# A first stage with its loads in another order, x turned by VectorE, five raw weight buffers and weights split ahead of scalings

## The chip, the cores and the metric

The kernel runs on one core of a Trainium2 chip. The metric is the time of one execution in microseconds on the device; the time of before is the median of three runs. A core has a matrix engine (TensorE, PE in the profile; its weight loads are PEld), three engines for other arithmetic (VectorE = DVE, ScalarE = ACT, GpSimd = POOL), a SyncE (SP) whose queue issues the DMAs, and DMA engines. Each engine works off its own queue of instructions; semaphores make them wait for each other. SBUF is the on-chip memory, PSUM the small memory that matmuls write to.

## The reference

One layer of a streaming encoder, for a prompt of 512 frames and a sample of 64 frames, width 2048, all in float32. Cut to what matters here:

```python
mod = jax.nn.silu(c) @ w_ada + b_ada                     # (2048) @ (2048, 6*2048), for two c
sh1, sc1, g1, sh2, sc2, g2 = split(mod, 6)
h = rmsnorm(x, norm1) * (1 + sc1) + sh1
proj = h @ w_in                                          # then gated linear attention, gated DeltaNet
x = x + g1 * (concat(o_a, o_b) @ w_out)
h = rmsnorm(x, norm2) * (1 + sc2) + sh2
x = x + g2 * conv_ffn(h)                                 # w_up, causal depthwise conv, w_down
y = rmsnorm(x, final_norm)
```

The first stage of the kernel, which the change touches, computes x transposed and its row norms, the first two of the six modulation parts (sh1 and sc1), h, and the first six column blocks of `h @ w_in` together with 32 narrow columns of it.

## The kernel before

Float32 products are made of two parts each: a weight tile w is split into wh (w rounded to the matmul's short form, by ACT) and wl = w - wh (by DVE), h likewise into hh and hl, and one product is wh hh + wh hl + wl hh, that is six matmuls of 288 columns (`mm6`, L744 and L746) for a tile of 128 rows by 128 columns. The 576 frames stand as two halves of 288 (256 of the prompt and 32 of the sample).

The stage is the method `head`. It works in this order.

- **x.** `x_load` brings x in five blocks of 128 rows (the fifth, the sample, has 64), each as four loads of 512 columns. `x_square` sums squares on ACT, `x_norm` makes 1/rms (DVE and POOL), `x_turn` transposes by PE in groups of four 128x128 tiles into a PSUM tile (tag g, two buffers), which is copied out to `xT` by ACT for even groups and by DVE for odd ones. `x_diag` puts the norms on a diagonal, and `x_lengths` multiplies by ones so that rb holds each frame's 1/rms in all partitions.
- **Modulation.** The 16 tiles of the width are taken in six groups of 2, 2, 3, 4, 3 and 2 tiles (`GROUPS`). `modulation(g)` multiplies silu(c) with the columns of `w_ada` of group g, eight steps (for part 1 and then part 0 of the modulation, four k-steps each); group 0 goes one step at a time, the others two. Its tiles come in buffers `hraw` (nine of 512 KB); `ada_fill` issues the next loads as soon as steps free buffers. After four steps the row is copied out by DVE (rw), transposed by PE (L2410), summed and joined with the bias (L991, L1167) and, for the scale part, with norm1 (L1173).
- **h.** `scale(k)` makes tmp = xT * s1 * rb on DVE (L765); `make(k)` adds the shift and rounds to hh on ACT (L772) and makes hl on DVE (L775).
- **Products.** The six column blocks (`EARLY`) are taken in three pairs for each group; pair j = 3 g + e/2 is pair e/2 of group g. `pair_load` brings a pair's raw weights into a buffer of tag raw (three of them; 256, 384 or 512 KB for groups of 2, 3 and 4 tiles), `w_ahead(n)` issues the loads of all pairs below n, and `pair_split` makes wh (ACT, L1139) and wl (DVE, L1141) in three buffers each. For each group the loop runs the first pair (e = 0) tile by tile together with the narrow product (L1262), then the pairs e = 2 and e = 4; `product` advances the next group's modulation step by step, and at its fourth step issues two scalings of the next group. The sums over groups are kept in SBUF (`sum_early`, L1150 and L1164).

What sets the order: all loads of this stage are issued by SP in the order in which the program traces them, and an issue whose buffer isn't free holds up those behind it. ACT and DVE run their queues in an order that follows the trace too, except that `high_priority(offset=80)` moves instructions ahead and `issue_after(ins)` (`after`) holds them behind `ins` on its engine. In `x_turn` the transposes are held behind the last modulation step (`summed`) and the copies behind a given square (`squared`). For groups from 1 on, the next group's narrow split and first pair's split are traced at the start of e = 4, and scalings are held behind them (`split_of`).

The buffers of tag xr (two of 512 KB in the same pool as raw) aren't used in this stage before its last group.

Of the kernel before, what the change touches and what calls it, by code (L numbers as in the profile page):

```python
# [16 lines left out]
P = 128  # L17
# [97 lines left out]
class Kern:  # L115
# [714 lines left out]

    def raw_late(self):

        pool, tag = self.raws.pop(0)
        self.raws.append((pool, tag))
        return pool.tile([P, 1024 if pool is not self.xp else NJ * P], F32, tag=tag, name=self.name("raw"))
# [21 lines left out]
    def head(self, pool):  # L857
# [5 lines left out]
        xt, ms, squared = {}, {}, []  # L863
# [9 lines left out]
        def x_square(b):  # L873
            n = P if b < 4 else TS
            ms[b] = pool.tile([P, 8], F32, tag="ms4", bufs=5, name=self.name("ms4"))
            for q in range(4):
                A.activation(junk[:n], xt[b][q][:n], AF.Square, scale=float(D) ** -0.5, accum_out=ms[b][:n, q:q + 1])
                squared.append(last())
# [18 lines left out]
        def x_turn(b):  # L897
            n = P if b < 4 else TS
            per = 4 if b < 4 else 8
            for k0 in range(0, KD, per):  # L900
                ps = self.pgt()[:, 0]
                for k in range(k0, k0 + per):
                    with self.tc.issue_after(summed[0]) if summed else nullcontext():
                        T.transpose(ps[:, (k - k0) * n:(k - k0 + 1) * n], xt[b][k // 4][:n, k % 4 * P:(k % 4 + 1) * P],
                                    self.c["ident"][:n, :n])
                even = k0 // per % 2 == 0
                put = (lambda o, x: A.activation(o, x, AF.Copy)) if even else V.tensor_copy
                ahead = 4 * b + (8 if k0 // per < 2 else 10)
                with self.tc.issue_after(squared[min(len(squared), ahead) - 1]):
                    if b < 4:  # L910
                        put(xT[:, k0:k0 + per, b // 2, (b % 2) * P:(b % 2 + 1) * P], ps.rearrange("p (k t) -> p k t", k=per))
                    else:
                        for h in range(2):
                            put(xT[:, k0:k0 + per, h, HP:HT], ps.rearrange("p (k h t) -> p k h t", k=per, h=2)[:, :, h])
# [9 lines left out]
        x_load(2)  # L924
# [35 lines left out]
        def modulation(g):  # L960
# [3 lines left out]
            for n0 in range(8 * g, 8 * g + 8, together):  # L964
# [13 lines left out]
                summed[:] = [last]  # L978
# [51 lines left out]
        for b in range(5):  # L1030
            if b < 4:
                x_norm(b + 1)
# [3 lines left out]
            x_diag(b)  # L1036
# [1473 lines left out]
```

## Time and profile before

| | |
|---|---|
| time, median of three runs (lowest, highest) | 2729.54 us (2727.57, 2734.78) |
| the profiled execution's own time | 2729.87 us |
| its span, first to last instruction | 2728.2 us |
| mean granted clock of PE | 0.997 |
| HBM read and written | 400.38 MB and 84.04 MB |
| DMA, mean over the span | 179 GB/s |

The span is what the profiler saw between the first and the last instruction; the execution's own time has 1.7 us more around it. "Granted clock" is the share of full speed that the throttle gave PE. In a table of stretches, each row gives the stretch, its length, then for each engine the busy time and the number of instructions, PE's granted clock, the mean busy share of the DMA engines (it can be over 1, since packets overlap) and what they moved in GB/s. In the timeline a row has the start, the time until the last of the merged instructions ended, engine, line, operation, out<-in, the number of instructions, and in brackets the engine's idle time before it and what ended it.

The chain of work that ended last, over the whole span, by engine:

```profile
PE 82%; DVE 8%; DMA 4%; issue 3%; ACT 2%; SPq 0%; POOL 0%; ACTq 0%; DVEq 0%; POOLq 0%
```

The first stage's loads, from the DMA issues up to 200 us: 40 loads of w_ada of 512 KB and 32 of 384 KB, x in 16 loads of 256 KB and four of 128 KB, and the weight pairs in loads of 128 to 256 KB, two for each pair.

### The profile page before, as it was taken

How to read it: one execution, taken by the hardware profiler on the slowest of the kernel's cores; microseconds unless marked ns; L12 is line 12 of the kernel's file. 1: busy time of each engine (PE TensorE's matmuls, PEld its weight loads, DVE VectorE, ACT ScalarE, POOL GpSimd, SP SyncE). 2: the span in 40 equal slices, each digit the busy share in tenths (PEclk: the TensorE clock that was granted, in tenths of full speed). 3: DMA queues.
4: the chain of work that ended last, by engine and by line, in shares of the span. 5: the costliest groups of instructions: out<-in, count | busy, mean ns of one | idle time of the engine just before them, and what ended most of it. 6: DMA issues, size and time to landing. Idle time of an engine off the chain costs nothing.

```text
span 2728.2 us, 52233 instructions
## 1 busy us (share of the span) xinstructions
PE 2682.6 (98%) x20208; PEld 2620.1 (96%) x20208; DVE 2292.2 (84%) x3747; ACT 1295.6 (47%) x2317; POOL 477.8 (18%) x461
## 2 busy tenths in 40 slices
PE   7999999999999999999999999999999999999998
PEld 5799999999999999999999999999999999999998
DVE  4579899988989895688999999999999976888996
ACT  4246454555554442554545454545454544333453
POOL 0001010110001000001333333333333300000241
PEclk9999999999999999999999999999999999999999
DMA  9986565555565583634555555555555595674762
GB/s 303 347 256 186 151 171 161 168 171 147 154 180 164 159 270 90 179 98 120 162 168 163 167 163 167 165 165 167 163 168 162 165 312 184 197 223 121 237 181 82
DMA packets 646203, 487.84 MB, mean 179 GB/s; under 512 B 66601, under 2 KB 568356, under 8 KB 645956
## 3 DMA queue, kind: packets, MB, share of 16 engines
q1 hardware_dynamic: 632852, 471.04, 57.5%
q10 hardware_dynamic: 13104, 13.47, 1.7%
q8 instruction: 159, 2.61, 0.4%
q14 instruction: 88, 0.72, 0.1%
HBM read 400.38 MB, written 84.04 MB: 178 GB/s over the span
## 4 chain that ended last, share of the span: by engine, by line
PE 82%; DVE 8%; DMA 4%; issue 3%; ACT 2%; SPq 0%; POOL 0%; ACTq 0%; DVEq 0%; POOLq 0%
PE g L744 17%; PE bank L1881 16%; PE bank L1880 16%; PE bank L1882 16%; PE g L746 8%; PE bank L2414 4%; DVE wl L1790 2%; PE bank L744 1%; PE bank L2410 1%; DVE m L2368 1%; DVE wl L2395 1%; DMA raw<-in_w_out_dram 1%; PE bank L973 1%; DMA raw<-in_w_in_dram 1%; DVE slot L2076 1%
## 5 line engine op out<-in xcount | busy, mean ns | idle before, releaser
L1881 PE MATMUL bank<-slot,wh 128*128 128x290 f32 (+1 forms) x3584 | 1067.3, 298 | 0.0
L1880 PE MATMUL bank<-slot,wh 128*128 128x290 f32 (+1 forms) x3584 | 1063.1, 297 | 1.0 <-DVE v L1903 0.6
L1882 PE MATMUL bank<-slot,wl 128*128 128x290 f32 (+1 forms) x3584 | 1060.3, 296 | 1.3 <-DVE wl L1790 1.2
L1882 PEld LDWEIGHTS bank<-slot,wl 128*128 128x128 f32 x3584 | 680.0, 190 | 2.9 <-DVE wl L1790 2.5
L1880 PEld LDWEIGHTS bank<-slot,wh 128*128 128x128 f32 x3584 | 675.4, 188 | 5.2 <-issue 4.4
L1881 PEld LDWEIGHTS bank<-slot,wh 128*128 128x128 f32 x3584 | 677.0, 189 | 0.1
L744 PE MATMUL g<-hh,wh 128*128 128x288 f32 x2048 | 470.1, 310 | 1.6 <-DVE kt L2395 0.7
L1788 ACT ACTIVATE wh<-raw 128x1024 fp32r<-128x1024 f32 (+1 forms) x304 | 280.7, 924 | 348.5 <-PE bank L1881 325.2
L746 PE MATMUL g<-hh,wl 128*128 128x288 f32 x2048 | 442.7, 297 | 2.3 <-DVE wl L1141 2.3
L744 PE MATMUL g<-hl,wh 128*128 128x288 f32 x2048 | 442.8, 297 | 0.3 <-DVE hl L775 0.2
L1790 DVE TENSOR_TENSOR wl<-raw,wh 128x1024 fp32r<-128x1024 f32 (+1 forms) x304 | 374.2, 1231 | 69.0 <-ACT wh L1788 66.0
L1788 ACT ACTIVATE wh<-s 128x1024 fp32r<-128x1024 f32 (+1 forms) x228 | 211.0, 927 | 296.5 <-PE bank L1881 136.6
L744 PEld LDWEIGHTS g<-hh,wh 128*128 128x128 f32 x2048 | 325.5, 189 | 15.9 <-issue 10.4
L746 PEld LDWEIGHTS g<-hh,wl 128*128 128x128 f32 x2048 | 330.8, 189 | 4.2 <-DVE wl L1141 2.7
L744 PEld LDWEIGHTS g<-hl,wh 128*128 128x128 f32 x2048 | 330.6, 189 | 2.7 <-issue 1.9
L1790 DVE TENSOR_TENSOR wl<-s,wh 128x1024 fp32r<-128x1024 f32 (+1 forms) x228 | 251.0, 1102 | 13.7 <-ACT wh L1788 12.5
L2395 ACT ACTIVATE wh<-raw 128x1024 fp32r<-128x1024 f32 x135 | 143.1, 1062 | 185.6 <-PE g L744 145.1
L2004 POOL TENSOR_TENSOR j<-j,j 128x288 f32<-128x288 f32 (+1 forms) x120 | 186.0, 1557 | 84.0 <-ACT j L2008 82.1
L2395 DVE TENSOR_TENSOR wl<-raw,wh 128x1024 fp32r<-128x1024 f32 x135 | 165.9, 1229 | 35.5 <-ACT wh L2395 35.2
L2395 DVE SCALAR_TENSOR_TENSOR acc<-aw,ct,acc 128x512 f32<-128x512 f32 x264 | 187.7, 743 | 0.0
L2395 DVE SCALAR_TENSOR_TENSOR acc<-xr,ct,acc 128x512 f32<-128x512 f32 x216 | 154.2, 748 | 0.0
L2076 DVE TENSOR_TENSOR slot<-bank,slot 128x288 f32<-128x288 f32 x184 | 83.0, 451 | 33.7 <-PE bank L1882 32.6
(317 smaller groups left out, 3269.4 us busy)
## 6 DMA issues: line engine op xcount, KB each, us to landing
raw<-in_w_up_dram SPq DMA_DIRECT2D x176, 512.0 KB
raw<-in_w_in_dram SPq DMA_DIRECT2D x100, 512.0 KB
raw<-in_w_down_dram SPq DMA_DIRECT2D x128, 320.0 KB
slot<-cd SPq DMA_DIRECT2D x140, 288.0 KB
aw<-in_w_ada_dram SPq DMA_DIRECT2D x74, 512.0 KB
cd<-j SPq DMA_DIRECT2D x120, 288.0 KB
xr<-in_w_ada_dram SPq DMA_DIRECT2D x54, 512.0 KB
hraw<-in_w_ada_dram SPq DMA_DIRECT2D x40, 512.0 KB
```

Source lines behind the costliest of these rows:

```text
L744: T.matmul(ps[:, h if bank is None else bank, :n], wh, x[:, h, :n], start=f, stop=False)
L746: T.matmul(ps[:, h if bank is None else bank, :n], wl, ah[:, h, :n], start=False, stop=stop)
L973: T.matmul(ps[32 * k:32 * k + 32, :w], cs[:, k0 + k], got[n][k // per][:, k % per], start=(n == together - 1 + 8 * g + 4 * (1 - mi)), stop ...
L1788: self.nc.scalar.activation(hi, src, AF.Copy)
L1790: self.nc.vector.tensor_tensor(lo, src, hi.bitcast(F32), op=ALU.subtract)
L1880: T.matmul(ps, wh[:, j], hi, start=(c < 3 and j == 0), stop=False, skip_group_check=True)
L1881: T.matmul(ps, wh[:, j], lo, start=False, stop=False, skip_group_check=True)
L1882: T.matmul(ps, wl[:, j], hi, start=False, stop=(j == n - 1), skip_group_check=True)
L2004: minus = lambda out, a, b: G.tensor_tensor(out, a, b, op=ALU.subtract)
L2076: V.tensor_tensor(dst, ps, dst, op=ALU.add)
L2395: r = f(*a, **kw)
L2414: return self.engine.matmul(out, *a, **kw)
```

## The change

- The constants are loaded first, then all five blocks of x (with the two c vectors behind the second), and only then `b_ada`, the norms, `w_ada` and weights. Of group 0, six `w_ada` tiles are issued, then weight pair 0 and the narrow weights, then the other two tiles, then pairs 1 and 2.
- A Silu of a small constant runs on ACT before the squares.
- `x_turn` copies the groups of the four prompt blocks by DVE alone, those of the sample block by ACT alone, and the holding behind `summed` and `squared` is gone. The modulation steps of group 0 come later in the trace: the first after block 3 is turned, the second before the lengths, three after them, the last three after the first two scalings.
- Weight pairs take five buffers: of each five, three of tag raw and two of tag xr. `w_ahead` runs two pairs further ahead throughout.
- In each group, the next group's narrow weights are loaded at the start; their split and the split of the next group's first pair are traced at the fourth modulation step, ahead of the two scalings, and the scalings are held behind them. Before, both splits stood at the start of e = 4.

```diff
+    def raw_early(self):
+        self.n_early = getattr(self, "n_early", -1) + 1
+        return self.xr() if self.n_early % 5 in (3, 4) else self.raw()
...
                 for k in range(k0, k0 + per):
-                    with self.tc.issue_after(summed[0]) if summed else nullcontext():
-                        T.transpose(ps[:, (k - k0) * n:(k - k0 + 1) * n], xt[b][k // 4][:n, k % 4 * P:(k % 4 + 1) * P],
-                                    self.c["ident"][:n, :n])
-                even = k0 // per % 2 == 0
-                put = (lambda o, x: A.activation(o, x, AF.Copy)) if even else V.tensor_copy
-                ahead = 4 * b + (8 if k0 // per < 2 else 10)
-                with self.tc.issue_after(squared[min(len(squared), ahead) - 1]):
...
+                    T.transpose(ps[:, (k - k0) * n:(k - k0 + 1) * n], xt[b][k // 4][:n, k % 4 * P:(k % 4 + 1) * P],
+                                self.c["ident"][:n, :n])
+                if b < 4:
+                    V.tensor_copy(xT[:, k0:k0 + per, b // 2, (b % 2) * P:(b % 2 + 1) * P], ps.rearrange("p (k t) -> p k t", k=per))
+                else:
+                    for h in range(2):
+                        A.activation(xT[:, k0:k0 + per, h, HP:HT], ps.rearrange("p (k h t) -> p k h t", k=per, h=2)[:, :, h], AF.Copy)
...
+        self.load_consts(self.cp, LONG)
         x_load(0)
-        self.load_consts(self.cp, LONG)
         x_load(1)
         v_load, v_turn = self.load_vectors()
         v_load(0)
-        x_load(2)
+        for b in range(2, 5):
+            x_load(b)
+        warm = pool.tile([P, 8], F32, tag="ms4", bufs=6, name=self.name("ms4"))
+        A.activation(warm, self.mhalf, AF.Silu)
+        for b in range(2):
+            x_square(b)
         v_turn(0)
...
-                    w_ahead(3 if g == 1 else 3 * g - 2)
+                    w_ahead(3 * g)
...
-        first, summed, self.split_of = modulation(0), [], None
-        ada_ahead(2)
-        x_load(3)
-        x_load(4)
-        ada_ahead(4)
+        first, self.split_of = modulation(0), None
         v_load(1)
-        ada_ahead(7)
+        ada_ahead(6)
         w_ahead(1)
         nar = self.narrow_load(*GROUPS[0])
-        x_square(0)
-        x_norm(0)
-        x_square(1)
+        ada_ahead(8)
+        w_ahead(3)
         for b in range(5):
-            if b < 4:
-                x_norm(b + 1)
             if b < 3:
                 x_square(b + 2)
             x_turn(b)
-            x_diag(b)
+            x_norm(b)
             if b > 0:
+                x_diag(b - 1)
+            if b == 3:
                 next(first)
-            if b == 3:
-                v_turn(1)
+        x_diag(4)
+        next(first)
         x_lengths()
+        v_turn(1)
+        for _ in range(3):
+            next(first)
         for k in range(2):
             scale(k)
...
-        w_ahead(2)
+        w_ahead(5)
...
+            nar_raw = None if end else self.narrow_load(*GROUPS[g + 1])
+
+            def split_next():
+                nonlocal nar
+                nar = self.narrow_split(pool, nar_raw)
+                begun.append(self.pair_split(*raws[3 * g + 3]))
+                self.split_of = last()
...
                     if stepped == 4 and not end:
+                        split_next()
                         for i in range(2):
                             scale(m0 + nm + i)
...
-                w = begun.pop(0) if begun else self.pair_split(*raws[3 * g + e // 2])
+                w = begun.pop(0) if e == 0 or g == 0 else self.pair_split(*raws[3 * g + e // 2])
...
-                            w_ahead(3 * g + 3)
+                            w_ahead(3 * g + 5)
...
-                    if e == 4 and not end and j == 0:
-                        nar = self.narrow_split(pool, self.narrow_load(*GROUPS[g + 1]))
-                        begun.append(self.pair_split(*raws[3 * g + 3]))
-                        self.split_of = last()
...
-                            w_ahead(3 * g + e // 2 + 3)
+                            w_ahead(3 * g + e // 2 + 5)
...
     def pair_load(self, offs, k0, n):
-        raw, w = self.raw(), n * P
+        raw, w = self.raw_early(), n * P
```

More of the change, by code (lines that the diff above doesn't have):

```diff
@@ L862, in head @@
         slot = lambda: self.hslot(places.pop(0), [P, 512])
-        xt, ms, squared = {}, {}, []
+        xt, ms = {}, {}
         last = lambda: nc.cur_bb.bb.instructions[-1]
@@ L874, in x_square @@
             n = P if b < 4 else TS
-            ms[b] = pool.tile([P, 8], F32, tag="ms4", bufs=5, name=self.name("ms4"))
+            ms[b] = pool.tile([P, 8], F32, tag="ms4", bufs=6, name=self.name("ms4"))
             for q in range(4):
                 A.activation(junk[:n], xt[b][q][:n], AF.Square, scale=float(D) ** -0.5, accum_out=ms[b][:n, q:q + 1])
-                squared.append(last())
         def x_norm(b):
@@ L977, in modulation @@
                     got[n] = None
-                summed[:] = [last]
                 ada_fill()
@@ L1016, in make @@
             self.h.append((hh, hl))
-        first, summed, self.split_of = modulation(0), [], None
-        ada_ahead(2)
-        x_load(3)
-        x_load(4)
-        ada_ahead(4)
+        first, self.split_of = modulation(0), None
         v_load(1)
-        ada_ahead(7)
+        ada_ahead(6)
         w_ahead(1)
         nar = self.narrow_load(*GROUPS[0])
-        x_square(0)
-        x_norm(0)
-        x_square(1)
+        ada_ahead(8)
+        w_ahead(3)
         for b in range(5):
-            if b < 4:
-                x_norm(b + 1)
             if b < 3:
```

4 lines of the change are left out of this document (removed).

## The prediction

> **What bounds the kernel now.** I read the page first (busy shares), then the table of stretches, then the PE waits of the first stage.
>
> ```profile
> PE 2682.6 (98%) x20208; PEld 2620.1 (96%) x20208; DVE 2292.2 (84%) x3747; ACT 1295.6 (47%) x2317; POOL 477.8 (18%) x461
> ```
>
> ```profile
> core 0: us, PE busy (x) PEld busy (x) DVE busy (x) ACT busy (x) POOL busy (x), PEclk, DMA share, GB/s
> 0.00:37.00 37.00, 21.17 (x162) 14.26 (x162) 13.78 (x45) 23.75 (x60) 3.78 (x12) 1.00 0.97 305
> 37.00:60.00 23.00, 22.34 (x185) 17.31 (x186) 8.87 (x23) 8.26 (x17) 0.26 (x1) 0.93 0.89 297
> 60.00:98.00 38.00, 35.20 (x273) 23.75 (x271) 21.79 (x48) 6.04 (x12) 0.59 (x2) 1.00 1.04 363
> 98.00:107.00 9.00, 6.95 (x41) 5.95 (x34) 4.79 (x9) 3.68 (x6) 0.00 (x0) 0.81 1.07 361
> 107.00:160.00 53.00, 53.00 (x449) 45.72 (x448) 33.04 (x69) 13.59 (x25) 0.21 (x1) 1.00 0.92 304
> 160.00:2728.20 2568.20, 2543.90 (x19113) 2513.11 (x19111) 2209.89 (x3557) 1240.26 (x2200) 472.94 (x445) 1.00 0.57 170
> ```
>
> TensorE (PE) is busy 98% of the span. The first stage (head) fills about 0 to 160 us; behind it PE is busy 2543.9 of 2568.2 us, and the change edits nothing there. So I take whatever the head gains or loses as passing to the end one for one. In the head there are three kinds of time to win. Before the first product (37 us) PE is idle 37.00 - 21.17 = 15.8 us. From 37 to 107 it is idle 0.66 + 2.80 + 2.05 = 5.5 us. From 107 to 160 it never rests: nothing can be won there. The third kind is half clock:
>
> ```profile
> 34.00:37.00 3.00, 0.63 (x6) 0.20 (x2) 2.42 (x8) 0.88 (x3) 0.00 (x0) 1.00 1.00 331
> 37.80:41.20 3.40, 3.40 (x19) 2.99 (x21) 2.09 (x5) 1.18 (x3) 0.00 (x0) 0.50 1.09 382
> 99.20:102.60 3.40, 1.67 (x12) 1.21 (x10) 2.42 (x3) 1.06 (x1) 0.00 (x0) 1.00 1.02 360
> 102.70:106.10 3.40, 3.40 (x16) 3.40 (x17) 1.10 (x4) 1.81 (x4) 0.00 (x0) 0.50 1.09 379
> ```
>
> Twice the granted clock is 0.50 for 3.4 us, each time right behind a stretch in which PE was busy half the time or less. Each costs half of 3.4 us, 1.7 us. So the most that can be won from 37 us on is 5.5 + 2 x 1.7 = 8.9 us, and the DMA column warns that not all of it is PE's own: from 60 to 107 us the DMA engines are full (share 1.04 and 1.07).
>
> ```profile
> PE g L746 <- DVE wl L1141: 2.3, 2, 2.1
> PE bank L2410 <- DVE rw L984: 1.5, 1, 1.5
> PE ps_nar L1262 <- ACT hh L772: 1.5, 1, 1.5
> PE g L744 <- ACT wh L1139: 0.5, 2, 0.3
> ```
>
> These are PE's longest waits from 37 to 162 us (total, times, longest): the split weights (wh, wl), the modulation row (rw), and hh, which is the start itself.
>
> **The start (0 to 37 us).**
>
> ```profile
> 12.27 1.28 ACT L931 ACT_TABLE_LOAD   x1
> 27.55 0.47 SPq L948 DMA_DIRECT2D hraw<-in_w_ada_dram  x1
> 28.01 0.64 PE L973 MATMUL bank<-hraw,cs 128*32 128x256 f32 x8
> 32.26 1.93 PE L973 MATMUL bank<-hraw,cs 128*32 128x256 f32 x32
> 33.05 1.81 DVE L765 SCALAR_TENSOR_TENSOR tmp<-xT,s,rb 128x512 f32<-128x512 f32 x4 [0.67 <-ACT rb L895]
> 34.78 0.41 DVE L984 COPY rw<-bank 128x256 f32<-128x256 f32 x1
> 36.12 1.81 ACT L772 ACTIVATE hh<-tmp,mod 128x512 fp32r<-128x512 f32 x4 [2.44 <-DVE mod L1167]
> ```
>
> ```profile
> L911 DVE COPY xT<-g 128x512 f32<-128x512 f32 x8 | 5.5, 690 | 7.8 <-PE g L904 7.8
> L907 ACT ACTIVATE xT<-g 128x512 f32<-128x512 f32 x8 | 4.7, 585 | 1.5 <-PE g L904 1.5
> ```
>
> The first product needs the eight modulation steps of group 0, hence their last load, issued at 27.55. Ahead of it stand all of x, the constants, c, b_ada, the norms, seven w_ada tiles, one weight pair and the narrow weights. Behind the change the same set stands ahead of it, only x earlier and w_ada later; the DMA share is already 0.97 up to 37 us. So that load lands when it landed, about 31 us by issue order and bytes, and the step that uses it still comes at about 32.3. Hence these edits cost or gain nothing:
> - The eight ACT copies become DVE copies: 8 x 0.69 = 5.5 us more on DVE, 4.7 us off ACT. DVE then has 13.78 + 5.5 = 19.3 us in 37, hidden under the loads. With that cover gone it would be up to 5.5 us.
> - The early Silu removes the 1.28 us table load in mid-stage; ACT isn't what ends last here. At most 1.28 us.
> - x and constants first: the two w_ada tiles that stood ahead of x's last blocks come behind, so the x chain (squares, lengths, rb) ends sooner, but it has to wait for the modulation.
>
> What does change is the tail. Now four steps run at 32.26 in 1.93 us, and rw waits until tmp ends at 34.86 although PE was done at 34.19. With the lengths done before, the steps follow their loads, and behind the last load stands one step of 0.64 us: 1.3 us less, and 0.5 us less for rw. Against it: PE now does little between the transposes and the last step, and both rows above show such a stretch being paid with half clock. I put 1.3 us for that (three quarters of one 1.7 us window). **Term 1: -1.8 + 1.3 = -0.5 us**, bounds -3.5 (x's earlier end also pulls the loads forward) and +2 (two half-clock windows, or DVE behind with x).
>
> The rule that speaks against the change here: the Trainium skill, TensorE: Matmul & The Clock Gate, Part 1, says that PE's clock falls to half after an idle window of about 3.4 us and recovers only after one busy window. This trace agrees with the length and the factor (3.40 us at 0.50). By the rule a sparser PE before the start gives one more such window, and the sum would be 0.4 us worse than with my three quarters.
>
> **Deeper weight loads and the middle (60 to 98 us).**
>
> ```profile
> 57.65 1.50 PE L973 MATMUL bank<-hraw,cs 128*32 128x384 f32 x16
> 59.97 3.98 SPq L948 DMA_DIRECT2D hraw<-in_w_ada_dram  x8
> 64.00 3.86 SPq L1126 DMA_DIRECT2D raw<-in_w_in_dram  x4
> 66.47 0.53 PE L746 MATMUL g<-hh,wl 128*128 128x288 f32 x2 [2.06 <-DVE wl L1141]
> 68.47 5.89 SPq L948 DMA_DIRECT2D hraw<-in_w_ada_dram  x8
> 77.50 3.62 SPq L1126 DMA_DIRECT2D raw<-in_w_in_dram  x2
> 81.37 6.25 SPq L948 DMA_DIRECT2D hraw<-in_w_ada_dram  x8
> 96.61 1.92 PE L973 MATMUL bank<-hraw,cs 128*32 128x512 f32 x16
> ```
>
> At 64.00 DVE scales the next x tiles (1.8 us) while wl waits behind it, and PE loses 2.06 us at 66.47. Splitting first removes that wait, and pairs loaded two ahead remove the waits on wh. But what is late next? PE frees the w_ada buffers at 57.65, the second half of group 2's tiles goes out at 59.97, then weights and group 3's tiles without a pause, the last batch by 87.6. In issue order these are 8 x 384 + 16 x 512 KB of w_ada and 1 MB of pairs, 12.6 MB; at 363 GB/s they take 34.7 us, so the last lands at about 95, and PE uses it at 96.61. This chain of full DMAs fixes the use at 96.61, whatever PE saves in between: PE would wait there instead. So the 2.80 us of this stretch count as nothing. The deeper loads even add to it: between 59.97 and the last batch now go weight pairs 5, 6 and 7 (256 + 384 + 384 KB), then pairs 7, 8 and 9 (384 + 384 + 512 KB), 256 KB more, 0.26 MB / 363 GB/s = 0.7 us. **Term 2: +0.7 us**; bounds -2.8 (the DMAs have slack after all) and +2.
>
> SP's queue: the narrow load moves from late in a group to its start, ahead of 16 w_ada issues; two issues of under 0.5 us each, with a DMA queue in backlog. Nothing. Were the queue empty they would cost 1 us a group.
>
> **The end of the full-DMA stretch (98 to 107 us).**
>
> ```profile
> 87.66 5.91 SPq L1126 DMA_DIRECT2D raw<-in_w_in_dram  x4
> 97.97 0.84 ACT L1139 ACTIVATE wh<-raw 128x768 fp32r<-128x768 f32 x1 [11.19 <-DMA raw<-in_w_in_dram]
> 99.60 1.06 ACT L1139 ACTIVATE wh<-raw 128x1024 fp32r<-128x1024 f32 x1 [0.79 <-DMA raw<-in_w_in_dram]
> 100.69 1.23 DVE L1141 TENSOR_TENSOR wl<-raw,wh 128x1024 fp32r<-128x1024 f32 x1 [0.89 <-ACT wh L1139]
> 101.83 0.68 DVE L984 COPY rw<-bank 128x512 f32<-128x512 f32 x1
> 102.57 1.07 PE L2410 MATMUL bank<-consts,rw 128*128 128x128 f32 x4 [1.53 <-DVE rw L984]
> ```
>
> Pairs 8 and 9 were issued at 87.66 behind the full queue, so wh, wl and then rw came late: 2.05 us of idle PE, and it brought the second half-clock window, 1.7 us. With the change pairs 8 and 9 are issued a group earlier, and the split of pair 9 comes early in its group: I count all 3.7 us, less 0.5 us, since the next w_ada tiles (group 4) still come through a queue that holds 0.7 us more. **Term 3: -3.2 us**; bounds -3.7 and 0.
>
> **Sum:** -0.5 + 0.7 - 3.2 = -3.0 us. The profiled execution took 2729.87 us (span 2728.2 and 1.7 around it); the median of the three runs, 2729.54, is 0.3 lower. Forecast from the median: **2726.5 us**, by -0.11%. 0.3% (8.2 us) is about what a measurement of this kernel tells from no change.
>
> **The rivals.**
> 1. *The DMAs have slack.* All of 8.9 us goes, and the start gains up to 3.5: 2717 to 2721. For it: PE waits from 60 to 98 are laid to DVE and ACT, not to w_ada. Against: DMA share 1.04 and 363 GB/s there.
> 2. *A split that holds the weight buffer in use* (slower). wh and wl have three buffers (L1136). The split of the next group's first pair is now traced before that of this group's second pair and, from group 2 on, takes the buffer of the pair that PE is multiplying. If it stands ahead on ACT's queue, it waits for PE, and the second pair's split waits behind it; PE then waits for both: 1.06 + 0.84 us and some 0.2 between, 2.1 us, in groups 2, 3 and 4, each followed by half clock as at 102.7 (1.7 us): 3 x 3.8 = 11.4 us. From the sum, 2726.5 + 11.4 = 2738. Queued behind that split are also hh of later tiles and, on DVE, the sums that free PSUM. It decides from 1 us a group, where the gain is eaten. For it: at 64.00 a wait of just this kind is seen, wl behind other work on DVE's queue. Against: the second pair's buffer is long free, so the program's order can put it first.
> 3. *The first stage is bound by its loads throughout.* The waits at 98 to 107 come back as waits for w_ada of group 4, and nothing is left: 2729.5.
> 4. *The change doesn't do what it says:* the splits carry a raised priority before and after, and may stay where they stood on DVE; then terms 2 and 3 fall away except the 0.7: 2729.7.
>
> **How the numbers follow.** Forecast with its small variants 0.38; rival 1 0.22; rival 2 0.17; rivals 3 and 4 0.23 together, all within 0.3%. Faster by over 0.3% (below 2721.3) 0.22, slower (above 2737.7) 0.17, the rest 0.61. The range takes in both ends: low 2717 (8.9 + 3.5 = 12.4 us off), high 2739 (rival 2 with a start that is worse by 1).
>
> **What would show it.** Term 1: the first products at about 36.6 instead of 37.15, x's copies all on DVE, no table load at 12 us. Term 2: no wait on wl at 66, but PE idle at the last w_ada step of group 2 or a DMA share over 1 up to there. Term 3: no wait for rw near 102 and no half-clock window. Rival 2 would show as PE waits on wh at the second pair of groups 2 to 4, with ACT ended by PE ahead of it. The prediction is wrong if the head's end (PE's first full stretch behind 160 us) moves by more than 8 us, or if it moves and the end does not.

## The result, and the profile after

| | before | after |
|---|---|---|
| time, median of 8 runs (lowest, highest) | 2729.05 us (2727.57, 2734.78) | 2739.06 us (2736.41, 2741.77) |
| ratio, 95% interval | | 1.0038 [1.0029, 1.0046] |
| the profiled execution: time, span | 2729.87, 2728.2 us | 2739.16, 2737.4 us |
| start of the first product (L744) | 37.47 us | 40.64 us |

The change made the kernel slower by 0.38%, some 10 us; forecast were 3 us less. One execution of the run one_ahead_held fell into a slow state of the chip (2872.77 us, granted clock 0.85) and is left out below. First the table of stretches of the changed kernel, cut as in the prediction (the columns are the same):

```profile
0.00:37.00 37.00, 23.55 (x160) 15.17 (x160) 16.15 (x45) 18.44 (x51) 3.78 (x12) 0.90 0.94 281
37.00:60.00 23.00, 19.05 (x157) 14.84 (x154) 9.34 (x25) 8.84 (x17) 0.27 (x1) 0.86 1.05 329
60.00:98.00 38.00, 32.32 (x245) 23.06 (x243) 20.10 (x43) 8.07 (x16) 0.58 (x2) 0.96 0.95 304
98.00:107.00 9.00, 8.93 (x67) 7.17 (x68) 5.05 (x14) 0.00 (x0) 0.00 (x0) 1.00 1.10 358
107.00:160.00 53.00, 49.13 (x406) 39.65 (x405) 29.27 (x62) 11.91 (x22) 0.21 (x1) 0.97 0.99 322
160.00:2737.40 2577.40, 2552.78 (x19184) 2522.49 (x19182) 2216.40 (x3569) 1243.30 (x2206) 475.79 (x445) 1.00 0.58 170
```

Read the second column, PE's busy time, against the first. From 98 to 107 us PE now works 8.93 of 9.00 us (6.95 before) at full clock: the one stretch that was to be won is won. But every other stretch of the stage is worse: 37 to 60 us 19.05 (22.34 before), 60 to 98 us 32.32 (35.20), 107 to 160 us 49.13 of 53 (53.00). The last two columns tell more: from 60 to 98 us the DMA engines were over-full before (1.04, 363 GB/s) and move less now (0.95, 304 GB/s); a second profile of before, of which more below, has 1.00 and 350 GB/s there.

I compared the start of the n-th product matmul (g<-h, counted from 0) in the two traces; there are 6144 records of this form, 36 for each tile of the width in this stage. After lags before by 3.17 us at matmul 0, 4.82 at 72 (start of group 1), 8.19 at 144 (group 2), 7.63 at 200, 6.39 at 252 (group 3), 9.88 at 400; at the end the span is 9.2 us longer. All of it arises in the first stage, and it passes to the end almost one for one.

PE's waits from 30 to 162 us in the changed kernel (total, times, longest), the complete list down to 0.9 us:

```profile
PE ps_nar L1267 <- ACT hh L772: 6.0, 4, 1.9
PE bank L2415 <- DVE rw L987: 4.2, 6, 0.8
PE bank L977 <- DMA hraw<-in_w_ada_dram: 3.4, 3, 2.0
PE g L744 <- DVE s L1178: 1.5, 1, 1.5
PE g L746 <- DVE wl L1146: 1.4, 2, 1.1
PE g L744 <- DVE acc L1169: 0.9, 1, 0.9
```

Three of them matter: for hh at the first narrow product of a group (once before, 1.5 us, the start; now four times), for rw (before 2.6 us, twice), and for w_ada itself, which was not in the list before. All three waits for w_ada lie at the start, up to 36.34 us; behind that PE waits for no w_ada tile in this trace. No wait for wh is left.

**The start.** PE's timeline of the changed kernel, behind x's part:

```profile
32.16 0.64 PE L977 MATMUL bank<-hraw,cs 128*32 128x256 f32 x8 [0.50 <-DMA hraw<-in_w_ada_dram]
34.83 0.64 PE L977 MATMUL bank<-hraw,cs 128*32 128x256 f32 x8 [2.02 <-DMA hraw<-in_w_ada_dram]
36.34 1.06 PE L977 MATMUL bank<-hraw,cs 128*32 128x256 f32 x8 [0.88 <-DMA hraw<-in_w_ada_dram]
37.94 0.69 PE L2415 MATMUL bank<-consts,rw 128*128 128x128 f32 x2 [0.54 <-DVE rw L987]
40.13 0.72 PE L1267 MATMUL ps_nar<-hh,nar 128*66 128x288 f32 x2 [1.50 <-ACT hh L772]
40.64 1.17 PE L744 MATMUL g<-hh,wh 128*128 128x288 f32 x4
```

The last three modulation steps of group 0 each wait for their w_ada tile, the last until 36.34; before, the last four ran at 32.26 without a wait. The SP queue and the stretches from 10 to 20 us show what changed ahead of that. SP's first w_ada issues, before and then after:

```profile
10.14 1.01 SPq L948 DMA_DIRECT2D hraw<-in_w_ada_dram  x2
18.16 1.02 SPq L948 DMA_DIRECT2D hraw<-in_w_ada_dram  x2
22.30 1.69 SPq L948 DMA_DIRECT2D hraw<-in_w_ada_dram  x3
```

```profile
19.34 4.05 SPq L952 DMA_DIRECT2D hraw<-in_w_ada_dram  x6
28.61 2.12 SPq L952 DMA_DIRECT2D hraw<-in_w_ada_dram  x2
```

With x alone in the queue, SP's x issues wait for earlier x loads to land, as its own list of waits shows (the same columns),

```profile
SPq L876 <- DMA hs<-in_x_prompt_dram: 3.9, 8, 1.4
```

and the DMAs move less. That this wait is the reason is not shown: before, the x issues waited too, 2.5 us in five times. The stretches of 5 us, before and then after:

```profile
10.00:15.00 5.00, 2.82 (x11) 1.87 (x11) 2.55 (x9) 4.88 (x13) 0.56 (x1) 1.00 0.90 292
15.00:20.00 5.00, 4.22 (x20) 2.93 (x23) 1.50 (x5) 4.29 (x13) 0.55 (x1) 1.00 1.08 363
```

```profile
10.00:15.00 5.00, 4.93 (x26) 3.49 (x25) 4.27 (x14) 3.21 (x11) 0.90 (x2) 1.00 0.97 273
15.00:20.00 5.00, 3.45 (x23) 2.38 (x24) 4.46 (x11) 4.78 (x15) 0.75 (x2) 1.00 0.91 256
```

5 us x (292 + 363 - 273 - 256) GB/s = 0.63 MB less has come in from 10 to 20 us, which is 1.8 us at 350 GB/s. This holds beyond one profile: from 15 to 20 us the eight profiles with the new load order move 226 to 256 GB/s, the twelve with the old one 317 to 370. But most of it is made up soon: from 0 to 37 us it is 274 to 291 GB/s with the new order and 270 to 305 with the old, and the profile of before that I compare with has the 305.

**The middle.** The steps of group 2's modulation, which free w_ada's buffers, before (the first of them, at 57.65, stands in the prediction) and then after:

```profile
60.59 1.50 PE L973 MATMUL bank<-hraw,cs 128*32 128x384 f32 x16
69.04 1.50 PE L973 MATMUL bank<-hraw,cs 128*32 128x384 f32 x16
71.42 1.50 PE L973 MATMUL bank<-hraw,cs 128*32 128x384 f32 x16
```

```profile
64.87 1.50 PE L977 MATMUL bank<-hraw,cs 128*32 128x384 f32 x16
67.16 1.50 PE L977 MATMUL bank<-hraw,cs 128*32 128x384 f32 x16
77.75 1.50 PE L977 MATMUL bank<-hraw,cs 128*32 128x384 f32 x16
80.52 1.50 PE L977 MATMUL bank<-hraw,cs 128*32 128x384 f32 x16
```

They are 6.6 to 9.1 us late. Not only the start is in that: counted in product matmuls, they stand behind 91, 96, 137 and 144 where before they stood behind 86, 96, 120 and 120. 144 is the end of group 1's products, so nothing covers the way from rw over the transposes and the bias to hh any more. While the buffers wait for such steps the DMAs move little: 88 GB/s from 55 to 60 us before, 182 and 204 in the two stretches from 60 to 70 us after (322 before). That gap is not the loss, though; it has only moved. Over 50 to 70 us both kernels move the same, before and then after:

```profile
50.00:70.00 20.00, 17.46 (x147) 12.91 (x150) 9.81 (x22) 4.96 (x10) 0.32 (x1) 1.00 0.79 254
```

```profile
50.00:70.00 20.00, 17.39 (x142) 13.20 (x141) 7.49 (x20) 7.26 (x14) 0.32 (x1) 0.91 0.83 253
```

Nor do the deeper weight loads make it: from 60 to 70 us the run a_order, without them, has 177 GB/s, the run b_five, which has them and the old start, 265, and the second profile of before 254.

The late steps cost at the group's end. In group 2 after catches up by its last product: it lags by 1.02 us at matmul 251, with one step (1.92 us) still to come that stood behind 216 products before and stands behind 252 now. Behind that step PE waits for rw (0.84 us) and for hh, and at matmul 252 the lag is 6.39 us:

```profile
109.04 1.92 PE L977 MATMUL bank<-hraw,cs 128*32 128x512 f32 x16
114.03 0.46 PE L1267 MATMUL ps_nar<-hh,nar 128*66 128x288 f32 x2 [1.57 <-ACT hh L772]
```

### The profile page after: what moved, and what is told of

It is laid out like the page before. It is cut to its first block, busy times and chain, and to the rows that moved or that the text cites. A ratio compares the mean times of both kernels' runs of the same rounds, so it can differ in the third digit from the quotient of the medians.

```text
span 2737.4 us, 52212 instructions
## 1 busy us (share of the span) xinstructions
PE 2685.8 (98%) x20208; PEld 2622.4 (96%) x20208; DVE 2296.3 (84%) x3753; ACT 1290.6 (47%) x2311; POOL 480.6 (18%) x461
## 4 chain that ended last, share of the span: by engine, by line
PE 83%; DVE 8%; issue 3%; DMA 3%; ACT 2%; SPq 1%; POOL 0%; ACTq 0%; DVEq 0%; POOLq 0%
PE g L744 17%; PE bank L1886 16%; PE bank L1885 16%; PE bank L1887 16%; PE g L746 8%; PE bank L2419 4%; DVE wl L1795 2%; DVE m L2373 1%; PE bank L2415 1%; PE bank L744 1%; PE bank L977 1%; DVE acc L2400 1%; DVE wl L2400 1%; DMA raw<-in_w_out_dram 1%; DVE slot L2081 1%
## 5 line engine op out<-in xcount | busy, mean ns | idle before, releaser
L744 PE MATMUL g<-hh,wh 128*128 128x288 f32 x2048 | 469.0, 310 | 2.4 <-DVE s L1178 1.5
L744 PE MATMUL g<-hl,wh 128*128 128x288 f32 x2048 | 443.6, 297 | 0.0
L744 PEld LDWEIGHTS g<-hh,wh 128*128 128x128 f32 x2048 | 325.5, 190 | 14.3 <-issue 11.3
L744 PEld LDWEIGHTS g<-hl,wh 128*128 128x128 f32 x2048 | 331.3, 189 | 1.1 <-issue 1.0
```

Of the source, the lines that this page charges most:

```text
L744: T.matmul(ps[:, h if bank is None else bank, :n], wh, x[:, h, :n], start=f, stop=False)
```

## The experiments

Theories, with the numbers that the expectations use (those that speak of others say in words what they mean): 3, w_ada comes late behind the deeper weight loads; 4, the modulation steps moved back in PE's queue; 5, the load order of the start; 6, half clock from a sparse PE at the start; 7, scalings held behind the early split; 8, the loads bind the whole first stage, and PE's waits and clock in it only follow.

| run | median us | ratio to before, 95% interval |
|---|---|---|
| a_order | 2732.99 | 1.0017 [1.0008, 1.0026] |
| b_five | 2732.91 | 1.0015 [1.0006, 1.0024] |
| ab_no_split | 2735.08 | 1.0026 [1.0015, 1.0036] |
| bc_no_order | 2734.26 | 1.0019 [1.0010, 1.0029] |
| a1_new_loads | 2732.61 | 1.0019 [1.0010, 1.0027] |
| a2_old_loads | 2732.83 | 1.0013 [1.0004, 1.0022] |
| bf_steps_held | 2730.80 | 1.0006 [0.9997, 1.0015] |
| as_scale_first | 2738.96 | 1.0035 [1.0023, 1.0048] |
| after_steps_held | 2738.75 | 1.0031 [1.0019, 1.0043] |
| bc_steps_held | 2732.36 | 1.0012 [1.0003, 1.0020] |
| one_ahead_held | 2728.06 | 0.9995 [0.9986, 1.0005] |
| after_kept_busy | 2737.72 | 1.0038 [1.0025, 1.0052] |
| a2_kept_busy | 2734.11 | 1.0021 [1.0012, 1.0030] |
| copies_only | 2729.38 | 1.0003 [0.9994, 1.0012] |
| best_kept_busy | 2728.71 | 1.0001 [0.9992, 1.0009] |
| less_loads | 2735.26 | 1.0022 [1.0013, 1.0031] |
| early_steps | 2731.66 | 1.0009 [1.0001, 1.0018] |

Each ratio is to executions of before from the run's own session, so it is not the quotient of two medians of this table.

**The parts of the change.** a_order keeps the load order, x's turn, the Silu and the steps of the start; b_five the five buffers and the deeper loads; ab_no_split both; bc_no_order all but the start.

```diff
  a_order, against the change: raw_early and split_next undone, and
-                    w_ahead(3 * g)
+                    w_ahead(3 if g == 1 else 3 * g - 2)
...
  b_five, against before (the other calls of w_ahead likewise):
-        w_ahead(2)
+        w_ahead(5)
...
-        raw, w = self.raw(), n * P
+        raw, w = self.raw_early(), n * P
...
```

> Only the load order and x's part of the change (constants and all of x first, VectorE alone turns x, the modulation steps of group 0 later); three raw buffers and the splits as before. Theory 1 (the loss of 9.4 us in the first stage is two losses: 3.2 us at the start, because the loads of x alone don't keep the DMA engines full, and some 6 us from the early split): first product at about 40.6 us as in the changed kernel, and the time about 3 us over before, 2732. Theory 2 (a late start is made good later, since the DMA engines run ahead of PE; the whole loss is the splits'): first product late too, but the time within 1 us of before.

> Only the five raw buffers and the weight loads two pairs further ahead; load order and splits as before. Theory 1: the wait for the late pairs at 98 to 107 us and its half-clock window go, 0 to 4 us faster than before, 2725 to 2729. Theory 3 (weight loads further ahead push the w_ada loads back in the full DMA queue, and PE waits for those): 3 to 6 us slower, with PE waits on the w_ada tiles between 60 and 110 us.

> The change without its early split: load order and five raw buffers as changed, the next group's splits at the start of e = 4 as before. Theory 1: the early split's 6 us go, 2729 to 2733. Theory 3: still 2736 to 2739, the split hardly matters.

> The change without its load order: five raw buffers and the early split, x and modulation of group 0 as before. Theory 1: start as before (first product at 37.5 us), the early split's loss stays, about 6 us slower than before, 2735; the wait for hh at the start of group 1 (1.9 us in the changed kernel) is there. Theory 2's opposite, that the loss is all in the late start: 2729.

Start and deeper loads cost about 4 us each, together 6. The early split adds 4 us to both (2739.06 against 2735.08) and 1.3 to b_five; for each of these two the intervals overlap. No part gains. The time of b_five is that of theory 3, but not its sign: its PE waits for w_ada only once, 0.7 us, at the start, and else for hh and rw. ab_no_split lies between its two forecasts and decides nothing.

**The start in two.** a1_new_loads changes the loads' order alone; a2_old_loads is a_order with before's.

```diff
  a1_new_loads, against before:
+        self.load_consts(self.cp, LONG)
         x_load(0)
-        self.load_consts(self.cp, LONG)
...
-        x_load(2)
+        for b in range(2, 5):
+            x_load(b)
...
-        ada_ahead(2)
-        x_load(3)
-        x_load(4)
-        ada_ahead(4)
         v_load(1)
-        ada_ahead(7)
+        ada_ahead(6)
...
+        ada_ahead(8)
+        w_ahead(3)
```

> Of the change only the order of loads (constants, all of x, then w_ada); x turned by both engines and steps of group 0 as before. Theory 5: first product at 40 to 41 us, time 2732 to 2734. Theory 6: first product at 37.5 to 38.5 us, time within 1 us of before.

> Of the change only VectorE turning x, the later steps of group 0 and the early Silu; loads in the order of before, three raw buffers, splits as before. Theory 5 (the start is late because x's small loads without w_ada among them leave the DMA engines short of work at 10 to 20 us): first product back at 37.5 us or up to 1 us earlier, time 2728 to 2730. Theory 6 (the loss at the start is VectorE's and PE's: one engine less to copy, steps later, half clock): first product at 40 to 41 us, time 2732 to 2734.

The load order alone costs 4 us: theory 5 holds for it. But so does the rest of the start with the old order, which theory 5 did not foresee, and the two don't add up in a_order. In the profile of a2_old_loads the first product comes at 38.20 us, 0.7 us behind that of before; the lag grows later, to 3.3 us at the start of group 2 and 4.5 at that of group 3, and PE waits for w_ada four times, 5.0 us. Half clock from a sparse PE is tested further down.

**Steps held, scalings first.** bf_steps_held is b_five with ten products held behind the steps that PE had ahead of them before; as_scale_first is the change with split_next behind the two scalings.

```diff
  bf_steps_held, against b_five:
+        held_behind = {15: 4, 16: 5, 20: 7, 28: 8, 30: 9, 36: 11, 43: 12, 44: 13, 49: 14, 53: 15}
...
-                self.mm6(ps[j]
+                n = held_behind.get(len(products))
+                products.append(k)
+                with self.after(None if n is None else steps_done[n]):
+                    self.mm6(ps[j]
```

> Five raw buffers and deeper weight loads alone, but the products are held behind the modulation steps at the places in PE's queue where these stand before (last step of group 1 behind 120 matmuls of the products, not 144; of group 2 behind 216, not 252). Theory 4 (the deeper loads cost because the program's order then puts the modulation steps at the end of each group: late buffers for w_ada, and nothing to cover the way from the last step to hh): PE's waits for hh at about 79.5 and 110.6 us go, 3 to 6 us faster than without the hold, 2727 to 2730. Theory 3 (weight pairs ahead of w_ada in a full DMA queue make the tiles land late): PE waits for w_ada tiles at the forced places instead, and the time stays at 2732 to 2735.

> The change with its two scalings traced ahead of the split again, so that they aren't held behind it. Theory 7 (the hold of the scalings behind the split makes hh of the next group late: waits of 1.9, 1.0 and 1.6 us at the starts of groups 1 to 3 and half clock behind them): the wait at about 59.7 us goes, 2 to 4 us faster than the change, 2735 to 2737. Theory 4: these waits come from the late last step of each group; no difference, 2738 to 2740.

PE's waits of b_five, then of bf_steps_held:

```profile
PE g L744 <- ACT hh L772: 3.0, 3, 1.8
PE bank L2415 <- DVE rw L989: 2.1, 3, 0.8
PE bank L978 <- DMA hraw<-in_w_ada_dram: 0.7, 1, 0.7
```

```profile
PE bank L978 <- DMA hraw<-in_w_ada_dram: 4.1, 4, 2.1
PE bank L2422 <- DVE rw L991: 3.0, 2, 2.4
PE g L744 <- ACT hh L772: 0.3, 1, 0.3
```

Held, the waits for hh go and by the medians half of the 4 us with them (the two intervals overlap); what takes their place is the wait for w_ada, 4.1 us against 0.7. The time lies just above theory 4's forecast and below theory 3's, and the waits show both at work: unheld, PE waits at the group's end, held, for the tiles. Theory 7 isn't borne out: with the scalings first the wait at 59.7 us goes (the lag at the start of group 1 is 3.3 us instead of 4.8), a wait for wl of 2.7 us comes instead, and the time is the same. With five executions the interval, 1.0023 to 1.0048, would still take in a win of 2 us.

**Holding in the whole change, and a shallower candidate.** after_steps_held adds the same holding to the change, bc_steps_held to bc_no_order. one_ahead_held is before with five buffers, pairs one further ahead (not two), and the holding.

```diff
  one_ahead_held, against before (besides raw_early and the holding):
-                            w_ahead(3 * g + 3)
+                            w_ahead(3 * g + 4)
...
-                            w_ahead(3 * g + e // 2 + 3)
+                            w_ahead(3 * g + e // 2 + 4)
```

> The whole change, with one thing added: in groups 0 to 2 ten of the product batches are held behind the modulation steps that PE had ahead of them in the kernel before, so that the modulation steps come at before's places in PE's queue. Theory 4 (what costs is that the deeper weight loads move the modulation steps back to the group's end, where nothing covers the path from rw to hh and where w_ada's buffers come free late): the waits of PE for hh (1.0 to 1.9 us each, three of them up to 115 us) and the half clock behind them go, some 4 us less than the change, 2735. Theory 3 (the loads themselves are late whatever the order): PE waits for w_ada instead and the time stays 2738 to 2739. Either way the first product stays where it is in the change (40.6 us), since the load order of the start is untouched.

> Five raw buffers, deeper weight loads and the early split, with the start (load order and x's copies) as in the kernel before, and the modulation steps held at before's places. If theories 4 and 5 are all there is (steps moved back, and the start's load order), nothing of the loss is left: 2728 to 2730, and the early split adds no more than 1 us to what the run without it (2730.8) took. If the early split costs by itself (theory 7), 2732 to 2735. If the deeper loads cost by w_ada being late (theory 3), 2731 with waits for w_ada of 4 us as in the run without the split.

> The kernel before with five raw buffers and the weight pairs only one further ahead, and only in the loop (the first loads and those at the start of a group's w_ada loads as before), modulation steps held at before's places. A candidate that may beat both: theory 3 (w_ada late behind the deeper weight loads) says that with 0.4 MB less ahead of w_ada the waits for w_ada shrink from 4 to about 2 us and the waits at 98 to 107 us (late pairs 8 and 9, 3.7 us with the half clock) still go: 2726 to 2728. If the full DMAs bind whatever the order: 2728 to 2730, same as before.

> The kernel before once more, for its profile: how far the speed of the loads and the place of the first product differ between two profiled executions of one kernel. If its 512 KB loads of w_ada take 1.4 us each from 33 to 45 us again and the first product stands at 37.5 within 0.3 us, the runs' head offsets can be read to that; if they take 1.5 us, offsets under some 2 us say nothing.

In the change the holding brings nothing that can be measured (2738.75): there PE waits for w_ada instead, in its list

```profile
PE bank L977 <- DMA hraw<-in_w_ada_dram: 6.5, 4, 2.9
```

against 3.4 us in the change. Theory 4's forecast of 2735 was a miss by the median, though the interval, 1.0019 to 1.0043, still takes it in. bc_steps_held lies in the range that its forecast gave for an early split that costs by itself, 1.6 us above bf_steps_held, but with overlapping intervals. With pairs one ahead nothing is lost, and nothing won either. The second profile of before explains why single profiles misled me; its PE timeline:

```profile
37.08 0.64 PE L973 MATMUL bank<-hraw,cs 128*32 128x256 f32 x8 [1.56 <-DMA hraw<-in_w_ada_dram]
38.26 0.44 PE L2410 MATMUL bank<-consts,rw 128*128 128x128 f32 x2 [0.55 <-DVE rw L984]
40.50 1.04 PE L744 MATMUL g<-hh,wh 128*128 128x288 f32 x4
```

The unchanged kernel starts its products at 40.50 here, 3.03 us later than in its first profile, behind a wait for a w_ada tile as in the changed kernel, yet this execution took 2731.38 us, 1.5 us more. So a shift of 3 us at the start proves nothing in one profile; the timed runs do.

**Clock and copies.** The kept_busy runs add transposes of the identity to PE where it only waits; copies_only changes who copies x.

```diff
  after_kept_busy, against the change (a2_kept_busy and best_kept_busy alike, at fewer places):
+        def busy(n, behind):
+            for q in range(n):
+                with self.tc.issue_after(behind):
+                    T.transpose(ps_nar[:, 0, q % 4 * P:(q % 4 + 1) * P], self.c["ident"], self.c["ident"])
+                behind = last()
...
  copies_only, against before:
-                even = k0 // per % 2 == 0
+                even = b == 4
```

> The whole change, with 39 transposes of the identity on PE that nobody reads: 10 around the turning of the sample block, 20 behind the last three modulation steps of group 0, 9 behind the last L2415 transposes, each where PE only waits. Theory 6 (PE is sparse before the first product and pays with half clock): the half clock at 22.8 to 29.6 and at 36.4 to 43.2 goes, mean granted clock of the executions from 0.994 to about 0.997, the first product 0.5 us earlier and the products behind it at full clock (1.3 us), 2 us less than the change: 2737. If half clock costs nothing there (hidden behind the loads), 2739.

> The changed turn of x and the later modulation steps with before's load order (2732.8), and 32 transposes of the identity on PE that nobody reads (10 around the turning of the sample block, 13 ahead of the last L2415 transposes, 9 behind). If half clock is what this part costs: the clock rises from 0.9953 to about 0.997 and the time falls to 2729 to 2730. If the later steps cost (w_ada's buffers of group 0 come free later, the next loads start later, waits for w_ada of 5 us): the clock rises and the time stays within 1 us of 2732.8.

> The kernel before with one edit: x's transposes are copied out by VectorE alone for the four prompt blocks, by ScalarE alone for the sample block; loads, steps, buffers and splits as before. The prediction priced this at nothing (5.5 us more on DVE, hidden under the loads). If that holds, 2729 within 1 us, and the first part's cost lies in the load order and the later steps. If VectorE's chain of copies delays the lengths and so the start: up to 2733.

> The candidate with weight pairs one further ahead and the modulation steps held (2728.7), and 15 transposes of the identity on PE that nobody reads, 6 ahead of the last transposes of the modulation row and 9 behind them, where PE waits 1.05 and 1.50 us. Theory 6: the half clock behind the first product (3.4 us, 1.7 us lost) goes: 2727, 2 us less than the kernel before. If the start is bound by the loads, what PE gains there it waits for w_ada later: 2728.5.

Two stretches of 6.8 us, first of the change, then of after_kept_busy (the seventh column is the granted clock):

```profile
22.70:29.50 6.80, 6.22 (x41) 3.94 (x45) 0.83 (x4) 2.32 (x8) 0.54 (x1) 0.50 1.07 352
36.40:43.20 6.80, 4.76 (x23) 3.49 (x24) 4.55 (x11) 2.85 (x6) 0.00 (x0) 0.50 1.09 349
```

```profile
22.70:29.50 6.80, 5.03 (x58) 2.86 (x56) 1.45 (x7) 2.53 (x8) 0.54 (x1) 1.00 1.08 339
36.40:43.20 6.80, 6.28 (x57) 5.27 (x55) 4.11 (x10) 3.38 (x7) 0.27 (x1) 1.00 1.09 349
```

The edit does what it should: 0.50 becomes 1.00, and the mean clock of all executions rises from 0.994 to 0.997. The ratio stays 1.0038, though with five executions its interval is wider than the 2 us that theory 6 promised. The same with a2 (0.9953 to 0.9971, 2732.8 to 2734.1, where 2729 to 2730 was forecast) and with the candidate (2728.06, 2728.71). Three times half clock is taken away and in none is time won that can be measured: theory 6's half clock is not what costs. The DMA share beside it is 1.07 to 1.09 in both kernels, which fits a stretch set by its loads. That PE then waits longer for loads is not shown: with the added transposes its waits for w_ada are shorter (2.6 us against 3.4, in a2 3.7 against 5.0). The copies cost nothing that can be measured, as forecast.

**The loads themselves.** less_loads leaves three w_ada loads of group 1 out of the change; early_steps puts group 0's steps of a2_old_loads back.

```diff
  less_loads, against the change:
+                if j in (9, 11, 13):
+                    got[j] = got[j - 1]
+                    continue
  early_steps, against a2_old_loads:
-            if b == 3:
+            if b > 0:
                 next(first)
...
-        for _ in range(3):
-            next(first)
```

> The whole change, with three of the 8 loads of w_ada of group 1 left out (1.57 MB; the steps use the tile before a second time, so the modulation of group 1 is computed from other data; its matmuls and all other work are as in the change). If the loads bind the first stage (theory 8): 1.57 MB at about 350 GB/s is 4.5 us, and the time falls by 3 to 4.5 us from the change's 2739, to 2734.5 to 2736. If PE's own waits at the group's end (hh, rw) set the time and the loads only follow: within 1 us of 2739.

> The changed turn of x with before's load order, as in the run that took 2732.8 (ratio 1.0013), but the modulation steps of group 0 at before's places in the loop (one behind each block from the second on). If the later steps are what this part costs, since they free w_ada's buffers later (theory 8): 2729 to 2730. If it is the turn itself: 2732 to 2733, as before this edit; VectorE's copies alone took 2729.4.

1.57 MB less is worth 3.8 us by the medians and 4.4 by the ratios (1.0038 less 1.0022; the intervals touch at 1.0029 to 1.0031). That is the size of theory 8, 4.5 us, while PE's work is the same in amount. It need not be the bytes alone: three tiles fewer also need three buffers fewer, and the steps of group 1's modulation stand behind 8, 8, 18 and 30 products instead of 12, 27, 41 and 58. Which of the three gave the time, no run tells apart. early_steps lies between its two forecasts, 1.2 us below a2_old_loads with overlapping intervals: inconclusive.

## Why the prediction was wrong

- **The head passes one for one to the end**: right, 9.9 us at product matmul 400 and 9.2 in the span.
- **Term 1, the start (-0.5 us)**: the failed step is "the same set stands ahead of it ... So that load lands when it landed". The same bytes stood ahead, but the DMAs moved 0.63 MB less from 10 to 20 us, and the last steps waited for w_ada. Over the seven profiles with before's load order and turn the first product comes at 37.47 to 40.50, mean 38.7; over seven with the new load order at 39.26 to 41.73, mean 40.5: 1.8 us late (the kept_busy runs, a2's, early_steps and copies_only aside; among these after_kept_busy, with the new order, has 38.15, and copies_only, with the old, 40.02). In time a1_new_loads puts it at 4 us. The term's tail was right but covered: that PE needs 0.64 us behind the last load helps little when that load is late. Half clock came, and more of it than the part of one 3.4 us window that I had counted: two stretches of 6.8 us. Its price, 1.3 us in the sum, did not show in the time.
- **Edits at nothing**: the copies held (1.0003 [0.9994, 1.0012]). "x and constants first" did not; it is term 1's miss. The early Silu and the earlier narrow load were in no run by themselves.
- **Term 2 (+0.7 us)**: "This chain of full DMAs fixes the use at 96.61, whatever PE saves" fits less_loads and the clock runs, but no trace of before or of the change shows PE waiting for w_ada there. The step that failed is to size only the 256 KB more in the queue. What I left out is that the order of PE's steps moves with the loads: in b_five the last steps of groups 1 and 2 stand behind 144 and 252 products, where they stood behind 120 and 216, and PE waits 3.0 us for hh behind them, against 0.3 before. b_five measures 3.8 us for it, over the bound of 2; the holding gives 2.1 of these back by the medians.
- **Term 3 (-3.2 us)**: the waits at 98 to 107 us went, as the prediction said, and so did the half clock. The lag falls only from 7.63 us at product matmul 200 to 6.39 at 252, 1.2 us, and is back at 9.88 at 400. The step that failed is to count the wait of PE as won without asking where the last step of the group then stands: it moved behind the group's last product, and what was won up to matmul 251 (a lag of 1.02 us) was lost again on the way from that step to hh. Putting the steps back by themselves (after_steps_held) doesn't win it either, since PE then waits for w_ada.
- **The rivals**: rival 2's number, 2738, is near the result, but not its mechanism: no wait for wh is left in the changed kernel's list; that the number is near is luck. Rival 4 is out, since the splits did move. Rival 3, the loads bind throughout, comes nearest; its sign, waits for w_ada, is seen in the changed kernel at the start only. I let it end at no change, because I asked only what of the gains would be left and not what the change does to the loads.

The Trainium skill, DMA: Bandwidth & Descriptors, Specifications, gives some 358 GB/s as the limit of HBM for one core. This case goes over that figure: before moved 363 GB/s from 60 to 98 us and 404 from 75 to 80. After moved 304 from 60 to 98 us, but 397 from 95 to 100, so it is not the reachable rate that the changed stage lacks.

**Open**: why the new load order starts the products late although most of the missing bytes are in by 37 us; why the changed turn with old loads costs about 4 us (not the clock, not the copies; the later steps perhaps 1.2 of it), why it and the load order don't add up, and what in the early split costs 1 to 4 us. That the loads bind the whole stage is in part argued: less_loads and the held runs fit it, the changed kernel's own waits do not show it. A tenth w_ada buffer, which would test theory 8 from the other side, wasn't tried.

## What to carry to other kernels

In a stage whose DMA share is at 1, price an edit by what it does to the loads: when each is issued, what stands ahead of it, and which instruction frees its buffer; here, taking away half clock in such a stage won nothing that could be measured. Prefetching one stream deeper in a shared queue can delay the other, and can move the instructions that use it to a place where nothing covers what follows them; look where they stand in the engine's queue, and not only at the wait that goes. A gap that lies in another place after a shift is not yet a loss: compare over a stretch that holds it in both kernels. Take a second profile of the unchanged kernel before building on a shift of 3 us.

## What the runs showed of the hardware

Removing half clock at the start in three kernels won no time that could be measured, as told above. And the granted clock did not follow PE's busy share. A stretch of the changed kernel, just ahead of its half clock from 22.8 us, and one of before, which was followed by full clock:

```profile
19.30:22.70 3.40, 2.38 (x24) 1.75 (x22) 2.35 (x7) 3.31 (x10) 0.94 (x2) 1.00 0.72 220
```

```profile
24.10:27.50 3.40, 1.83 (x16) 1.37 (x14) 1.85 (x5) 2.27 (x6) 0.25 (x1) 1.00 1.10 375
```

2.38 us busy was followed by half clock, 1.83 was not (I laid these stretches by the places where the clock changes; the profile doesn't show what the throttle counts). The first holds the sample's 64x64 transposes, the second only 128x128 ones; that the size of the matmuls counts is a guess, no run varied it.
